# First loads cut and split over two queues, the last gate moved, normed operands and squares moved to VectorE, and a transpose split in a decoder trunk

## The chip, the core and the metric

The kernel runs on one core of a Trainium2 chip. A core has five engines that work side by side and meet at semaphores: TensorE (PE, matmuls and transposes), VectorE (DVE), ScalarE (ACT), GpSimd (POOL) and SyncE (SP, which here only issues DMAs). Data lies in SBUF, matmuls write to PSUM. Each engine runs its own instructions in the order in which they were put in its queue. The metric is the device time of one execution in microseconds.

## What is computed

A two-layer decoder trunk over 256 tokens of width 1024, all in float32: a Mamba-2 layer, a gated FFN with a short causal convolution, dilated attention with a shared K/V, a second such FFN, and a final RMS norm.

```python
x = x + _mamba2_mixer(_rms_norm(x, a_norm[i]), ssm_w_in[i], ...)   # z, x, B, C, dt; conv; SSD; gate; group norm; w_out
x = x + _conv_ffn(_rms_norm(x, ffn_norm[layer]), ffn_w_up[layer], ffn_conv_w[layer], ffn_w_down[layer])
k_sh, v_sh = _shared_kv(x, kv_norm, w_kv, positions)
x = x + _dilated_mixer(_rms_norm(x, b_norm[j]), k_sh, v_sh, att_w_q[j], att_w_o[j], positions)
x = x + _conv_ffn(...)
return _rms_norm(x, final_norm)
```

## The kernel before

The stream X is held transposed, as 8 tiles of 128 channels by 256 tokens. Every float32 matmul is made of three matmuls on rounded parts: an operand is split in a high part (`xh`, `wh`, rounded by a cast) and a low part (`xl`, `wl`, the rest by a subtraction), and the products high-high, low-high and high-low are summed in PSUM (L270 to L272, L290 to L292, L660 to L668). ScalarE makes the casts (L96) and VectorE the subtractions (L98), 1024 columns at a time.

The weights come through the class `Weights`: a fixed sequence of units of 1 MB, three raw buffers, six pairs of `wh` and `wl`, each unit fetched one unit ahead of its use. `begin` (L144) loads the first two units in five pieces (512, 512, 1024, 1024, 1024 columns), with pieces of x between them, all issued by SP. The order on TensorE is written out by hand; on the other engines a scheduler puts the instructions in order ahead of time, by their place in the program and by when it thinks that they are ready, and that order is then fixed.

The stages around the change:

- The start: five pieces of weights and x, `hi_lo` (L184) on each tile of x times the norm's weight, the first matmuls of `z_pair`, then the norm's statistics and dt. `chunk_sums` (L447, tile `pac`) needs a chain of small VectorE operations on dt.
- The Mamba layer: a loop over 8 groups g. In it `conv_mm` for xs and for B and C, and the SSD of earlier groups, each cut in parts: `ssd_b` (transposes `px`), `ssd_a` (`pg`, then `gs` by ScalarE), `ssd_m` (GpSimd multiplies `dec` by `gs`, L531), `ssd_c` (`yo`, `py`, then a chain through VectorE, GpSimd and ScalarE that ends in `y` at L580), and `ssd_d` (transposes of `y` into `pt`, L588, then `hi_lo` into `yy`). The gates of groups 4 to 7 (`z_mm`, L387, in two halves of 24 matmuls, and `z_post`) stand in groups 1, 3, 5 and 7. In group 7 `ssd_d(5)` and `ssd_c(6)` stand between the halves (L630 to L636).
- `res_proj` (L641): w_out, w_down of the first FFN, and w_o. For the first tiles of outputs the last rows of k are put last (`late`), and `hooks` put other work after a given count of steps; a step is three matmuls, for one output tile and one k. When an output tile is done VectorE adds it to X (L680), and `Stream.add` makes the next stage's operands (L187) and adds its square to a sum (`add_sq`, L224).
- The FFNs (`ffn`, L708): 22 tiles of two halves. The first five tiles use operands without the norm's row factor, and the factor is put in afterwards (`u`, L724). From the sixth (j = 5) on, the operands are `normed` (L319, tiles `xnh` and `xnl`). After each tile come the conv steps (L314), the gate (L729) and the split of the result (L734).
- Attention: for each head h three `q_tile`s (24 matmuls each), `p_transpose(h - 2)` between the first and the second, then `values` for a pair of heads, then `scores(h - 1)`. `p_transpose` turns the probabilities in two blocks (c = 0: `p`, two transposes, copied by ScalarE; c = 1: `pm`, three, copied by VectorE).

Of the kernel before, what the change touches and what calls it, by code (L numbers as in the profile page):

```python
# [53 lines left out]
def trunk(ctx, tc, a, out):  # L54
# [17 lines left out]
    def load_x(i):  # L72
        SP.dma_start(out=X[:, 2 * i:2 * i + 2, :], in_=a["x"][:, 2 * i:2 * i + 2, :])
# [27 lines left out]
    class Weights:  # L101
# [42 lines left out]
        def begin(self, load, operand):  # L144

            raw = [wp.tile([128, 2048], F32, tag="raw", bufs=RB, name="raw") for _ in range(2)]
            whl = [[wp.tile([128, 1024], F32R, tag=t, bufs=WB, name=t) for t in ("wh", "wl")]
                   for _ in range(4)]
            cols = [slice(0, 512), slice(512, 1024), slice(1024, 2048), slice(2048, 3072),
                    slice(3072, 4096)]  # L150

            def part(t, c):
                return t[c.start // 2048][:, c.start % 2048:c.start % 2048 + c.stop - c.start]

            for i, c in enumerate(cols):
                if i != 1:
                    load(max(i - 1, 0))
                SP.dma_start(out=part(raw, c), in_=part([q[1] for q in self.seq], c))
            SP.dma_start(out=wdt.rearrange("p k h -> p (k h)"), in_=a["w_dt"])
            for i, c in enumerate(cols):  # L160
                wh, wl = (t[:, c.start % 1024:c.start % 1024 + c.stop - c.start]
                          for t in whl[c.start // 1024])
                if i == 0:
                    operand(0)
                elif i > 1:
                    operand(2 * i - 2)
                ACT.copy(out=wh, in_=part(raw, c))
                DVE.tensor_tensor(out=wl, in0=part(raw, c), in1=wh.bitcast(F32), op=ALU.subtract)
                if i == 0:
                    operand(1)  # L170
                elif i > 1:
                    operand(2 * i - 1)
            self.got += [whl[:2], whl[2:]]
# [10 lines left out]
    def hi_lo(xh, xl, x, w):  # L184

        ACT.activation(out=xh, in_=x, func=AF.Copy, scale=w)
        DVE.scalar_tensor_tensor(out=xl, in0=x, scalar=w, in1=xh.bitcast(F32),  # L187
                                 op0=ALU.mult, op1=ALU.subtract)
# [35 lines left out]
    def add_sq(acc, k):  # L224
        if k == 0:
            ACT.activation(out=acc, in_=X[:, 0, :], func=AF.Square)
        else:
            sq = wk.tile([128, T], F32, tag="sq", name="sq")
            ACT.activation(out=sq, in_=X[:, k, :], func=AF.Square)  # L229
            POOL.tensor_tensor(out=acc, in0=acc, in1=sq, op=ALU.add)  # L230
# [88 lines left out]
    def normed(w, rb):  # L319
# [3 lines left out]
        for k in range(KT):  # L323
            t = wk.tile([128, T], F32, tag="sq", name="xnt")
            ACT.activation(out=t, in_=X[:, k, :], func=AF.Copy, scale=P(w)[:, k:k + 1])
            POOL.tensor_tensor(out=t, in0=t, in1=rb, op=ALU.mult)
            ACT.copy(out=h[:, k, :], in_=t)
            POOL.tensor_tensor(out=l[:, k, :], in0=t, in1=h[:, k, :].bitcast(F32), op=ALU.subtract)
# [21 lines left out]
    W.begin(load_x, lambda k: hi_lo(xh[:, k, :], xl[:, k, :], X[:, k, :], P("a_norm")[:, k:k + 1]))  # L350
# [247 lines left out]
    for g in range(NG):  # L598
# [31 lines left out]
        if g in ZAT:  # L630
            z_mm(ZAT[g], 0)
            if g == NG - 1:
                ssd_d(g - 2)
                ssd_c(g - 1)
            z_mm(ZAT[g], 1)
            z_post(ZAT[g])  # L636
    ssd_b(NG - 1)
# [3 lines left out]
    def res_proj(w, nk, operand, late, S, first=2, hooks={}):  # L641
# [42 lines left out]
        while n0 < KT:  # L684
# [12 lines left out]
            for k in last:  # L697
# [6 lines left out]
    res_proj("w_out", 16, lambda k: yy[k // 2][:, k % 2 * 2:k % 2 * 2 + 2, :], [14, 15], S,  # L704
             first=4, hooks={20: lambda: ssd_d(NG - 2), 24: lambda: ssd_c(NG - 1), 52: lambda: ssd_d(NG - 1)})
# [164 lines left out]
    def q_tile(h, st, g):  # L870
# [3 lines left out]
        tile_a(po[:, g % 2, :], st["us"][g], xh, xl)  # L874
        if g:
# [39 lines left out]
    def p_transpose(h, st):  # L915


        if h % 2 == 0:
            pair[h // 2] = act.tile([128, 2, 640], F32, tag="xh0", name="pts")
        pts = pair[h // 2]  # L920
        for c in range(2):
# [26 lines left out]
    for h in range(AH):  # L948
        q_start(h, hs[h])
        q_tile(h, hs[h], 0)  # L950
        if h > 1:
            p_transpose(h - 2, hs[h - 2])
        q_tile(h, hs[h], 1)
# [216 lines left out]
```

## Time and profile before

| what | value |
|---|---|
| time, median of 3 runs | 779.81 us (777.24 to 781.5) |
| the profiled execution | 777.25 us |
| its span, first to last instruction | 775.5 us |
| TensorE busy | 761.5 us, 98% |
| VectorE busy | 604.4 us, 78% |
| ScalarE busy | 470.1 us, 61% |
| GpSimd busy | 146.2 us, 19% |
| read from HBM | 133.17 MB, 174 GB/s over the span |

A matmul row's duration is longer than the distance to the next matmul, since matmuls are pipelined; so starts are to be compared, not durations. A number in square brackets at the end of a timeline row is the time that the engine stood idle before it, with what ended that time.

### The profile page before, as it was taken

The numbers are of one execution on the slowest core, as the hardware profiler recorded it, in microseconds if no ns is written. First come the engines' busy times: TensorE is split into PE (matmuls) and PEld (weight loads), VectorE is DVE, ScalarE is ACT, GpSimd is POOL, SyncE is SP. The second block draws the span as 40 slices with busy tenths as digits, with TensorE's granted clock in tenths as the row PEclk, the third lists the DMA queues.
The fourth block names the chain that finished last, engine by engine and source line by source line (L and its number), as shares of the span: only waits on it lengthen the run. The fifth ranks groups of instructions, "written<-read, shape, count | busy, mean of one in ns | idle before, by whom it ended". The sixth has DMA issues, their size and how long they took to land.

```text
span 775.5 us, 14630 instructions
## 1 busy us (share of the span) xinstructions
PE 761.5 (98%) x5832; PEld 721.9 (93%) x5832; DVE 604.4 (78%) x1008; ACT 470.1 (61%) x793; POOL 146.2 (19%) x142
## 2 busy tenths in 40 slices
PE   8999999989999999999999999999999999999996
PEld 7899999989989999999888998989999999999885
DVE  5989988887496999887677598777587999888452
ACT  6757777775566676565556446556376767655331
POOL 0003626354216100000111132111125200000000
PEclk9999999999999999999999999999999999999998
DMA  8584753434173565545556554253234565554621
GB/s 308 212 300 170 283 174 110 164 109 158 61 272 110 173 233 202 207 151 173 184 200 236 194 189 147 101 187 118 105 115 158 191 224 212 184 197 141 220 75 54
DMA packets 22772, 135.72 MB, mean 175 GB/s; under 512 B 2544, under 2 KB 3600, under 8 KB 8624
## 3 DMA queue, kind: packets, MB, share of 16 engines
q1 hardware_dynamic: 21216, 130.03, 48.2%
q10 hardware_dynamic: 1488, 4.75, 1.8%
q8 instruction: 46, 0.75, 0.4%
q14 instruction: 22, 0.18, 0.1%
HBM read 133.17 MB, written 1.61 MB: 174 GB/s over the span
## 4 chain that ended last, share of the span: by engine, by line
PE 89%; DVE 4%; issue 2%; ACT 2%; DMA 1%; POOL 1%; SPq 0%; POOLq 0%; DVEq 0%
PE po L270 18%; PE po L271 17%; PE po L272 17%; PE po L660 7%; PE po L668 4%; PE po L662 4%; PE fo L1030 2%; PE fo L1028 2%; PE fo L1029 2%; PE py L565 2%; DVE wl L98 2%; PE po L290 1%; PE po L291 1%; PE po L292 1%; DMA raw<-w_z 1%
## 5 line engine op out<-in xcount | busy, mean ns | idle before, releaser
L98 DVE TENSOR_TENSOR wl<-raw,wh 128x1024 fp32r<-128x1024 f32 (+1 forms) x238 | 296.2, 1250 | 77.9 <-ACT wh L96 73.8
L96 ACT CAST wh<-raw 128x1024 fp32r<-128x1024 f32 (+1 forms) x238 | 245.0, 1040 | 184.3 <-PE po L271 99.1
L270 PE MATMUL po<-xnh,wh 128*128 128x256 f32 x800 | 226.6, 283 | 0.0
L272 PE MATMUL po<-xnh,wl 128*128 128x256 f32 x800 | 226.1, 283 | 0.0
L271 PE MATMUL po<-xnl,wh 128*128 128x256 f32 x800 | 225.3, 282 | 0.0
L270 PEld LDWEIGHTS po<-xnh,wh 128*128 128x128 f32 x800 | 150.9, 189 | 0.4 <-issue 0.2
L271 PEld LDWEIGHTS po<-xnl,wh 128*128 128x128 f32 x800 | 151.0, 189 | 0.0
L272 PEld LDWEIGHTS po<-xnh,wl 128*128 128x128 f32 x800 | 150.1, 188 | 0.1
L270 PE MATMUL po<-xh,wh 128*128 128x256 f32 x400 | 114.7, 287 | 0.0
L271 PE MATMUL po<-xl,wh 128*128 128x256 f32 x400 | 113.0, 282 | 0.5 <-DVE xl L187 0.5
L272 PE MATMUL po<-xh,wl 128*128 128x256 f32 x400 | 113.1, 283 | 0.0
L314 DVE SCALAR_TENSOR_TENSOR cv<-po,prm,cv 128x255 f32<-128x255 f32 (+2 forms) x232 | 106.2, 477 | 5.4 <-ACT cv L310 2.8
L270 PEld LDWEIGHTS po<-xh,wh 128*128 128x128 f32 x400 | 76.1, 190 | 1.6 <-issue 1.5
L271 PEld LDWEIGHTS po<-xl,wh 128*128 128x128 f32 x400 | 76.1, 190 | 0.7 <-DVE xl L187 0.7
L272 PEld LDWEIGHTS po<-xh,wl 128*128 128x128 f32 x400 | 75.8, 190 | 0.0
L660 PE MATMUL po<-gp,wh 128*128 128x512 f32 x176 | 61.4, 392 | 0.0
L230 POOL TENSOR_TENSOR sqacc<-sqacc,sq 128x256 f32<-128x256 f32 x21 | 21.4, 1019 | 211.5 <-ACT sq L229 211.2
L662 PE MATMUL po<-gp,wl 128*128 128x256 f32 x176 | 49.3, 280 | 0.0
L660 PEld LDWEIGHTS po<-gp,wh 128*128 128x128 f32 x176 | 33.0, 187 | 7.5
L1028 PE MATMUL fo<-wh,gp 128*128 128x512 f32 x88 | 34.5, 392 | 0.0
L1030 PE MATMUL fo<-wl,gp 128*128 128x512 f32 x88 | 34.5, 392 | 0.0
L1029 PE MATMUL fo<-wh,gp 128*128 128x512 f32 x88 | 34.5, 392 | 0.0
(226 smaller groups left out, 1283.0 us busy)
## 6 DMA issues: line engine op xcount, KB each, us to landing
raw<-w_up SPq DMA_DIRECT2D x44, 1024.0 KB, 4.8
raw<-w_down SPq DMA_DIRECT2D x18, 1024.0 KB, 4.8
raw<-w_xs SPq DMA_DIRECT2D x8, 1024.0 KB, 6.2
raw<-w_bc SPq DMA_DIRECT2D x8, 1024.0 KB, 5.5
raw<-w_out SPq DMA_DIRECT2D x8, 1024.0 KB, 4.9
raw<-w_q SPq DMA_DIRECT2D x8, 1024.0 KB, 5.1
raw<-w_z SPq DMA_DIRECT2D x6, 1024.0 KB, 6.0
dec<-rows ACTq DMA_DIRECT2D x8, 512.0 KB, 5.3
```

What stands on the lines that cost most here:

```text
L96: ACT.copy(out=wh[:, :n], in_=raw)
L98: DVE.tensor_tensor(out=wl[:, :n], in0=raw, in1=wh[:, :n].bitcast(F32), op=ALU.subtract)
L270: PE.matmul(po, lhsT=wh, rhs=xh, start=start, stop=False, **kw)
L271: PE.matmul(po, lhsT=wh, rhs=xl, start=False, stop=False, **kw)
L272: PE.matmul(po, lhsT=wl, rhs=xh, start=False, stop=stop, **kw)
L314: r = DVE.scalar_tensor_tensor(out=dst[:, i, s:], in0=u[:, i, :T - s], scalar=w[i][:, taps - 1 - s:taps - s], in1=dst[:, i, s:], op0=ALU.m ...
L660: PE.matmul(p.rearrange("p c t -> p (c t)"), lhsT=wh[:, c], rhs=y.rearrange("p c t -> p (c t)"), start=st, stop=False, skip_group_check=True)
L662: PE.matmul(p[:, 1, :], lhsT=wl[:, c], rhs=y[:, 0, :], start=False, stop=sp, skip_group_check=True)
L668: PE.matmul(p[:, o, :], lhsT=l[:, c], rhs=y[:, x, :], start=st and q == 0 and not o, stop=sp and q == 2, skip_group_check=True)
L1028: PE.matmul(po[c], lhsT=x[:, 0, t], rhs=wh[:, o], start=k == 0, stop=False)
L1029: PE.matmul(po[c], lhsT=x[:, 1, t], rhs=wh[:, o], start=False, stop=False)
L1030: PE.matmul(po[c], lhsT=x[:, 0, t], rhs=wl[:, o], start=False, stop=k == FT - 1)
```

## The change

It has four parts. First, x is loaded in pieces of 1, 1, 2, 2, 2 tiles instead of 2, 2, 2, 2, each ahead of its piece of weights, and the first two pieces of weights are issued by ScalarE's queue. The first tile's high part is made by VectorE. Second, both halves of the last gate and its `z_post` stand ahead of `ssd_d(5)` and `ssd_c(6)`, and in w_out four instead of two rows of k are put last, with the hooks of `ssd_c(7)`, `ssd_d(6)` and `ssd_d(7)` moved. Third, `normed` makes its product by one VectorE operation instead of ScalarE's and GpSimd's two, and its low part by VectorE; `add_sq` adds on VectorE. Fourth, `p_transpose` turns its second block after four of the eight k of the second `q_tile`.

```diff
     def load_x(i):
-        SP.dma_start(out=X[:, 2 * i:2 * i + 2, :], in_=a["x"][:, 2 * i:2 * i + 2, :])
+        k = slice(i, i + 1) if i < 2 else slice(2 * i - 2, 2 * i)
+        SP.dma_start(out=X[:, k, :], in_=a["x"][:, k, :])
...
             for i, c in enumerate(cols):
-                if i != 1:
-                    load(max(i - 1, 0))
-                SP.dma_start(out=part(raw, c), in_=part([q[1] for q in self.seq], c))
+                load(i)
+                (SP if i > 1 else ACT).dma_start(out=part(raw, c), in_=part(src, c))
...
-                if i == 0:
-                    operand(0)
-                elif i > 1:
+                if i < 2:
+                    operand(i)
+                else:
                     operand(2 * i - 2)
                 ACT.copy(out=wh, in_=part(raw, c))
                 DVE.tensor_tensor(out=wl, in0=part(raw, c), in1=wh.bitcast(F32), op=ALU.subtract)
-                if i == 0:
-                    operand(1)
-                elif i > 1:
+                if i > 1:
                     operand(2 * i - 1)
...
-    def hi_lo(xh, xl, x, w):
-        ACT.activation(out=xh, in_=x, func=AF.Copy, scale=w)
+    def hi_lo(xh, xl, x, w, dve=False):
+        if dve:
+            DVE.tensor_scalar(out=xh, in0=x, scalar1=w, scalar2=None, op0=ALU.mult)
+        else:
+            ACT.activation(out=xh, in_=x, func=AF.Copy, scale=w)
...
             ACT.activation(out=sq, in_=X[:, k, :], func=AF.Square)
-            POOL.tensor_tensor(out=acc, in0=acc, in1=sq, op=ALU.add)
+            DVE.tensor_tensor(out=acc, in0=acc, in1=sq, op=ALU.add)
...
             t = wk.tile([128, T], F32, tag="sq", name="xnt")
-            ACT.activation(out=t, in_=X[:, k, :], func=AF.Copy, scale=P(w)[:, k:k + 1])
-            POOL.tensor_tensor(out=t, in0=t, in1=rb, op=ALU.mult)
+            DVE.scalar_tensor_tensor(out=t, in0=X[:, k, :], scalar=P(w)[:, k:k + 1], in1=rb,
+                                     op0=ALU.mult, op1=ALU.mult)
             ACT.copy(out=h[:, k, :], in_=t)
-            POOL.tensor_tensor(out=l[:, k, :], in0=t, in1=h[:, k, :].bitcast(F32), op=ALU.subtract)
+            DVE.tensor_tensor(out=l[:, k, :], in0=t, in1=h[:, k, :].bitcast(F32), op=ALU.subtract)
...
-        if g in ZAT:
+        if g in ZAT and g < NG - 1:
             z_mm(ZAT[g], 0)
-            if g == NG - 1:
-                ssd_d(g - 2)
-                ssd_c(g - 1)
             z_mm(ZAT[g], 1)
             z_post(ZAT[g])
+    z_mm(7, 0)
+    z_mm(7, 1)
+    z_post(7)
+    ssd_d(NG - 3)
+    ssd_c(NG - 2)
     ssd_b(NG - 1)
     ssd_a(NG - 1)
     ssd_m(NG - 1)
...
-    res_proj("w_out", 16, lambda k: yy[k // 2][:, k % 2 * 2:k % 2 * 2 + 2, :], [14, 15], S,
-             first=4, hooks={20: lambda: ssd_d(NG - 2), 24: lambda: ssd_c(NG - 1), 52: lambda: ssd_d(NG - 1)})
+    res_proj("w_out", 16, lambda k: yy[k // 2][:, k % 2 * 2:k % 2 * 2 + 2, :], [12, 13, 14, 15], S,
+             first=4, hooks={24: lambda: (ssd_c(NG - 1),), 30: lambda: (ssd_d(NG - 2),), "k12": lambda: (ssd_d(NG - 1),)})
...
         q_tile(h, hs[h], 0)
         if h > 1:
-            p_transpose(h - 2, hs[h - 2])
-        q_tile(h, hs[h], 1)
+            p_transpose(h - 2, hs[h - 2], (0,))
+        q_tile(h, hs[h], 1, range(4))
+        if h > 1:
+            p_transpose(h - 2, hs[h - 2], (1,))
+        q_tile(h, hs[h], 1, range(4, KT))
```

## Rows read from the trace of the kernel before

**Rows 1.** The page, part 4: the chain that ended last, by engine.

```profile
PE 89%; DVE 4%; issue 2%; ACT 2%; DMA 1%; POOL 1%; SPq 0%; POOLq 0%; DVEq 0%
```

**Rows 2.** Waits of PE: who waited for whom: us in total, times, longest.

```profile
PE ptr L924 <- DVE pm L910: 1.4, 4, 0.4
...
PE pac L451 <- DVE smalls L441: 0.6, 1, 0.6
PE po L271 <- DVE xl L187: 0.5, 1, 0.5
```

**Rows 3.** Timeline of 0 to 17 us: start, us, engine, line, op, tiles, [idle before].

```profile
0.73 1.28 ACT L423 ACT_TABLE_LOAD   x1 [0.73 <-PEq L1162]
...
1.63 0.91 SPq L158 DMA_DIRECT2D raw<-w_z  x2
...
12.43 1.05 ACT L167 CAST wh<-raw 128x1024 fp32r<-128x1024 f32 x1 [0.39 <-DMA raw<-w_z]
...
14.79 0.19 PEld L292 LDWEIGHTS poz<-wl,xh 128*128 128x128 f32 x1 [0.56 <-DVE wl L168]
```

**Rows 4.** Busy time by stretch: PE, PEld, DVE, ACT, POOL; clock; DMA share, GB/s.

```profile
1.00:4.00 3.00, 2.95 (x14) 2.95 (x15) 0.19 (x2) 1.24 (x2) 0.00 (x0) 1.00 0.49 155
4.00:14.40 10.40, 9.29 (x32) 6.96 (x31) 6.19 (x10) 8.32 (x16) 1.29 (x1) 1.00 0.99 338
...
566.00:584.00 18.00, 17.54 (x147) 17.33 (x146) 18.00 (x24) 14.42 (x27) 6.34 (x7) 1.00 0.51 172
588.00:609.00 21.00, 21.00 (x175) 20.91 (x174) 16.43 (x26) 15.89 (x33) 13.39 (x16) 1.00 0.33 114
```

**Rows 5.** Timeline of PE, 168.9 to 181.4 us.

```profile
171.70 0.28 PE L292 MATMUL po<-wl,xnh 128*128 128x256 f32 x1
174.07 0.95 PE L588 MATMUL pt<-cst,y 128*128 128x128 f32 x4 [2.09 <-ACT y L580]
...
176.00 1.55 PE L565 MATMUL py<-xdt,dec 128*128 128x64 f32 x12 [0.16 <-POOL dec L531]
177.36 0.36 PE L290 MATMUL po<-wh,xnh 128*128 128x256 f32 x1
...
180.29 0.60 PE L542 MATMUL px<-cst,cv 128*128 128x128 f32 x4
...
181.30 0.37 PE L668 MATMUL po<-yy,wh 128*128 128x256 f32 x1
```

**Rows 6.** Timelines of ACT and of POOL, 145 to 210 us.

```profile
173.51 0.91 ACT L580 ACTIVATE y<-y,rs 128x256 f32<-128x256 f32 x2 [0.26 <-POOL rs L578]
...
185.40 3.53 POOL L531 TENSOR_TENSOR dec<-dec,gs 128x512 f32<-128x512 f32 x2 [0.98 <-ACT gs L524]
```

**Rows 7.** Timelines of PE (487.5 to 492.5) and of DVE (464 to 496).

```profile
488.01 0.38 PE L924 MATMUL ptr<-cst,p 128*128 128x128 f32 x2
488.80 0.52 PE L924 MATMUL ptr<-cst,pm 128*128 128x128 f32 x3 [0.40 <-DVE pm L910]
...
489.62 0.54 DVE L926 COPY pts<-ptr 128x384 f32<-128x384 f32 x1
```

**Rows 8.** Groups of DVE by form, 236 to 262: busy us, mean ns.

```profile
L314 DVE SCALAR_TENSOR_TENSOR cv<-u,prm,cv 128x254 f32<-128x254 f32 x6 | 5.1, 877 | 0.0
```

**Rows 9.** Timeline of DVE, 18 to 48 us.

```profile
30.40 0.48 DVE L343 SCALAR_TENSOR_TENSOR xnt<-X,prm,rbc 128x256 f32<-128x256 f32 x1
```

**Rows 10.** Groups of DVE by form, 566 to 584.

```profile
L187 DVE SCALAR_TENSOR_TENSOR xl<-X,prm,xh 128x256 fp32r<-128x256 f32 x8 | 6.6, 833 | 0.0
L680 DVE TENSOR_TENSOR X<-po,X 128x256 f32<-128x256 f32 x8 | 3.1, 415 | 2.4 <-PE po L668 2.4
```

**Rows 11.** Timelines of ACT (239 to 262), DVE (605 to 610), PE (607.9 to 608.9).

```profile
256.56 0.41 ACT L327 CAST xnh<-xnt 128x256 fp32r<-128x256 f32 x1 [1.32 <-POOL xnt L326]
...
607.33 1.22 DVE L98 TENSOR_TENSOR wl<-raw,wh 128x1024 fp32r<-128x1024 f32 x1
...
608.60 0.39 PE L272 MATMUL po<-xnh,wl 128*128 128x256 f32 x1
```

More of the change, by code (lines that the diff above doesn't have):

```diff
@@ L153, in part @@
                 return t[c.start // 2048][:, c.start % 2048:c.start % 2048 + c.stop - c.start]
+            src = [q[1] for q in self.seq]
             for i, c in enumerate(cols):
-                if i != 1:
-                    load(max(i - 1, 0))
-                SP.dma_start(out=part(raw, c), in_=part([q[1] for q in self.seq], c))
+                load(i)
+                (SP if i > 1 else ACT).dma_start(out=part(raw, c), in_=part(src, c))
             SP.dma_start(out=wdt.rearrange("p k h -> p (k h)"), in_=a["w_dt"])
@@ L348, in operands @@
         return h, l
-    W.begin(load_x, lambda k: hi_lo(xh[:, k, :], xl[:, k, :], X[:, k, :], P("a_norm")[:, k:k + 1]))
+    W.begin(load_x, lambda k: hi_lo(xh[:, k, :], xl[:, k, :], X[:, k, :], P("a_norm")[:, k:k + 1], k == 0))
     W.fetch(3)
@@ L868, in q_start, with q_tile @@
         st["us"] = W.get("w_q", h, 0) + W.get("w_q", h, 1)
-    def q_tile(h, st, g):
+    def q_tile(h, st, g, ks=range(KT)):
         if g != 1:
@@ L873, in q_tile @@
         po = st["po"]
-        tile_a(po[:, g % 2, :], st["us"][g], xh, xl)
-        if g:
+        tile_a(po[:, g % 2, :], st["us"][g], xh, xl, ks=ks)
+        if g and ks[-1] == KT - 1:
             gs = slice(0, 2) if g == 1 else slice(2, 3)
@@ L913, in trunk, with p_transpose @@
     pair = {}
-    def p_transpose(h, st):
-        if h % 2 == 0:
+    def p_transpose(h, st, cs=(0, 1)):
+        if h % 2 == 0 and cs[0] == 0:
             pair[h // 2] = act.tile([128, 2, 640], F32, tag="xh0", name="pts")
         pts = pair[h // 2]
-        for c in range(2):
+        for c in cs:
             pt = ps.tile([128, 512], F32, tag=f"t{3 + c}", name="ptr")
```

## The prediction, made before the change was run

> **What bounds the kernel now.** I read the chain of work that ended last first: 89% of it is TensorE and 4% VectorE, so time can only come out of places where TensorE stands still [rows 1]. The second view is therefore the list of what TensorE waited for. It is short: beside the long stall at the last gate (below) it has four waits of the probabilities' transposes (`ptr`) for `pm`, one of `pac` at 44 us and one of a matmul on `xl` of 0.5 us [rows 2]. That list counts a gap from the modelled end of a matmul, so I take the price of a stall from starts in the timeline instead. The changed parts sit on these stalls and on the start; no edit removes a matmul. One level step is useful: half a gate (24 matmuls) runs from 177.36 to 180.29, 2.93 us, so one 256-column matmul takes 0.122 us [rows 5].
>
> **First loads.** At 14.79 TensorE waits for the `wl` of the fourth piece of weights, whose cast starts at 12.43 when its DMA lands [rows 3]. So the fourth piece's landing sets the end of this stage, and not the first matmul. The DMA engines are 0.49 busy from 1 to 4 us and 0.99 busy after [rows 4]: first the single issuing queue limits, then the transfers do. The change moves two weight issues to ScalarE's queue and adds one x load, so on SP the fourth piece moves up by one issue, 0.91 / 2 = 0.46 us [rows 3]. That is also the value I take, 0.5. Filling the 3 us from 0.49 to 0.99 would be 1.5 us, the far end. The other end is a loss: ScalarE begins at 0.73 with a table load of 1.28 us [rows 3], and if its two issues stand behind it the first piece comes about half a microsecond later than now. The first normed operand goes to VectorE; this moves the first matmul only, which isn't the limit, and costs nothing. What is late next is `pac`, which already waits 0.6 us for VectorE [rows 2]; VectorE's chain there starts from TensorE's own results, so I let the gain pass.
>
> The row says 0.99 busy after 4 us. The Trainium skill (DMA: Bandwidth & Descriptors, Issuing engines are not separate DMA queues) speaks against a larger gain: queues of different engines run on the same 16 DMA engines, and a second one saves issue time only. By that rule the far end of 1.5 falls away and the half microsecond stays; the trace agrees as far as it goes.
>
> **The last gate whole ahead of group 5's turning.** Now the second half of gate 7 stands behind `ssd_d(5)` and `ssd_c(6)`. TensorE's last matmul of the first half starts at 171.70, the transposes of `ssd_d(5)` at 174.07; less 0.12 that is 2.25 us of stall for `y` of group 5, which ScalarE ends at 173.51 + 0.91 = 174.42 [rows 5, 6]. The four transposes behind the stall take 0.95 us where the four of `px` take 0.60: 0.35 more [rows 5]. With the second half put first, TensorE is busy until 171.82 + 2.93 = 174.75, when `y` is there: both go. The third loss is `py`, whose fifth matmul starts at 176.00 when `dec` is there [rows 5]. It could have started four transposes, two `yo` and four `py` after 174.07 + 0.35, at 174.42 + 0.44 + 0.43 + 0.45 = 175.74: 0.26 lost. After the change the same count from 174.75 gives 176.07, so `dec` is there and this goes too. The sum is 2.25 + 0.35 + 0.26, say 2.8 us. `z_post` only moves up and hides beside matmuls.
>
> `w_out` then starts at 178.5 instead of 181.30. Its first three units are split ahead of that; group 6 is now wanted after 48 steps instead of 37, which covers the later `ssd_d(6)`. What is late next is `ssd_c(7)`: 24 steps of 3 matmuls, 8.8 us, put it at 187.3. Its `dec` came from GpSimd at 185.40 + 3.53 = 188.93 [rows 6]. That multiply waits for `gs`, which comes from `ssd_a(7)`, now 2.8 us earlier, so it should move along. If it doesn't, 1.6 us are given back. I take none; bounds 1.2 to 2.9 us gained.
>
> **Probabilities turned in two places.** In head 3 the first block's transposes start at 488.01, the second block's at 488.80; two transposes take 0.22, so 0.57 us are lost for `pm`, of which the list shows 0.40 [rows 7]. The list has four such waits with 1.4 us [rows 2]: three like this one and one with 0.2. With the 0.17 that the list leaves out of each, it is 3 x 0.57 + 0.37 = 2.1 us. After the change 12 matmuls, 1.46 us, stand between the two blocks, more than twice the wait. The other side of the cover: VectorE's copy of the second block (489.62 for 0.54 [rows 7]) is needed by `values`, now 24 matmuls behind it, from then on 12. From the end of the turned block, 488.23 + 1.46 + 0.33 = 490.0, to `values` at 491.5 there are 1.5 us for 0.54. If VectorE takes a split first, 1.2 us by [rows 11], 0.3 is lost, in three heads 0.9. I take 2.1 and keep 1.2 as the low end. A further switch between kinds of matmul is added per head; at 180.29 transposes follow a gate's matmuls with no gap [rows 5], so I price it at nothing.
>
> **Normed operands and squares on VectorE.** In each FFN GpSimd loses eight multiplies and eight subtractions and ScalarE eight scalings. VectorE gains 8 x (0.48 + 0.42) = 7.2 us: the multiply is the row of L343, the subtraction the mean of L680, both 128x256 [rows 9, 10]. It also gets something back. While GpSimd works, VectorE's operations are longer: six conv steps of 128x254 average 0.877 us between 236 and 262, where one of the same kind and size takes 0.48; that is 2.4 us from this group alone [rows 8, 9]. So the load grows by at most 4.8 us, and VectorE has 21.00 - 16.43 = 4.6 us idle in the like stretch of the second FFN [rows 4]. It just fits, with a thin cover: the `wl` of tile 5 ends at 607.33 + 1.22 = 608.55, and the matmul that reads it starts at 608.60 [rows 11]. For the change speaks that ScalarE stood 1.32 us at 256.56 for GpSimd's multiply with weight casts queued behind [rows 11]; that wait goes. Against it: the subtraction on VectorE now waits for ScalarE's cast, splits and conv steps are queued behind it on VectorE, and TensorE waits for the splits. I take 0.25 us lost in each FFN; bounds 0.1 gained and 3 lost.
>
> The squares: in the last projection VectorE is busy 18.00 of 18 us, and TensorE loses 0.5 us for the last `xl` [rows 2, 4]. Eight `xl` take 0.833 each instead of 0.48, so 2.8 us come back [rows 9, 10]; of seven additions of 0.42 six stand ahead of the last `xl`, 2.5. The difference is 0.3; I take 0.4 gained, since a stretched split comes back too. Bounds 0.6 either way. In the other two projections TensorE never waited, and matmuls hide the additions; uncovered they are 2.9 us each.
>
> The rows show VectorE's operations up to twice as long beside GpSimd's. The Trainium skill (SBUF — State Buffer, Who interferes with whom) says that a VectorE instruction with two SBUF inputs and a GpSimd instruction that reads SBUF exclude each other for the whole instruction. By that rule GpSimd's own time comes back to VectorE and its load would not grow; that belongs to the third rival. The trace bears out the lengthening, not the full amount.
>
> **The sum.** 0.5 + 2.8 + 2.1 + 0.4 - 0.5 = 5.3 us. The profiled execution took 777.25 us (span 775.5 and 1.75 around it), which would become 772.0. The median of the three runs is 2.56 above the profiled one; the three spread over 4.3 us, and nothing in the profile prefers an end, so I take the gain off the median: 779.8 - 5.3 = 774.5.
>
> **Rivals.** First, half is given back: `ssd_c(7)` waits 1.6 for `dec`, the start gains nothing (0.5), `values` waits 0.9. The gain is 2.3, the time 777.5. For it: each new cover is 1 to 1.5 us thick. Against it: GpSimd's multiply follows `ssd_a`, which moves too.
>
> Second, VectorE becomes the bound in the FFNs; this is the slow side. The subtractions wait for ScalarE and tile 5's split comes late. TensorE feels it as soon as VectorE is 0.05 us later at 608.5 than now. The other edits gain 5.8, so it decides from 2.9 us in each FFN, and beyond the measurable from 4.9. At 3 in each the time is 780.0; with no relief and no idle time used, 7.2 each, it is 779.8 + 14.4 - 5.8 = 788.4.
>
> Third, the loads gain the full 1.5 and the FFNs 0.1 each: 7.0, 772.8. It needs full DMA engines from 1 us on.
>
> Last, the start does not do what it says, ScalarE issuing behind its table load: 0.5 lost instead of gained, 775.5, inside the forecast's spread.
>
> **How the numbers follow.** The forecast with its spread (773 to 776.5) gets 0.52, half given back 0.25, VectorE as the bound 0.15, the larger gain 0.08. A measurement of this kernel can tell about 0.5% from no change, 3.9 us: 775.9 and 783.7. Faster: 0.08 and nearly all of 0.52 make 0.58 (some of the spread lies above 775.9). Slower: over half of 0.15, 0.09. The rest, 0.33, is the same. The range reaches from the larger gain on the profiled execution's footing, 770.5, to the mild form of VectorE's bound, 781.
>
> **What would show it.** Right: no wait of `pt` at 172, `w_out` starting about 3 us sooner, no wait of `ptr`, conv steps near 0.48 at the start of both FFNs, no `xl` wait after the last projection. Wrong: TensorE waiting for `wl` or `xnl` near 256 to 262 or 605 to 612, for `dec` near 187, for `pts` ahead of `values`, or `pac` waiting longer by what the start gained.

## The result and the profile after

The changed kernel takes 771.69 us (median of five, 771.42 to 773.9) against 779.81 us; the ratio is 0.9899 with an interval of 0.9877 to 0.992. It is faster, as forecast, and inside the range; the time forecast was 774.5 us, with a spread of 773 to 776.5, and the measured time lies 1.3 us below that spread. By medians the gain is 8.1 us, between the two profiled executions only 5.6 us (777.25 to 771.69). The forecast was 5.3. The distance between 5.6 and 8.1 is the main question of what follows.

The engine shares of the chain of work that ended last, of the kernel after [rows 1]:

```profile
PE 93%; issue 2%; DVE 2%; ACT 1%; DMA 1%; POOL 1%; SPq 0%; POOLq 0%; DVEq 0%
```

The waits of TensorE after [rows 2]: who waited for whom, us in total, times, longest.

```profile
PE warm L90 <- DVE nhalf L269: 1.1, 1, 1.1
PE poz L293 <- ACT wh L169: 0.8, 1, 0.8
PE poz L295 <- DVE wl L170: 0.7, 2, 0.5
PE pac L454 <- DVE smalls L444: 0.7, 1, 0.7
PE poz L293 <- DVE xh L187: 0.4, 1, 0.4
PE pg L522 <- ACT cv L419: 0.3, 1, 0.3
PE po L673 <- DVE OT L950: 0.2, 1, 0.2
```

The waits of `pt`, `ptr`, `xl` and of `py` for `dec` are gone, as forecast; `pac` still waits, and `pg` for `cv` is new. The new wait stands between the transposes `px` and `w_out` in TensorE's timeline (start, us, line, tiles, idle before in brackets) [rows 5]:

```profile
174.34 0.60 PE L591 MATMUL pt<-cst,y 128*128 128x128 f32 x4
...
177.13 0.61 PE L545 MATMUL px<-cst,cv 128*128 128x128 f32 x4
178.06 0.70 PE L522 MATMUL pg<-cv 128*128 128x256 f32 x2 [0.33 <-ACT cv L419]
...
178.74 0.48 PE L673 MATMUL po<-yy,wh 128*128 128x256 f32 x2
```

ScalarE's timeline says why: three weight casts stand in its fixed order ahead of the `cv` that `pg` reads [rows 6].

```profile
174.18 2.94 ACT L98 CAST wh<-raw 128x1024 fp32r<-128x1024 f32 x3
177.02 0.47 ACT L189 ACTIVATE yy<-pt,prm 128x256 fp32r<-128x256 f32 x1
177.39 0.62 ACT L419 ACTIVATE cv<-cv 128x512 f32<-128x512 f32 x1
```

Starts of the same TensorE instruction in the two profiled executions give the gain stage by stage:

| TensorE starts | before | after | gained so far | in this stage |
|---|---|---|---|---|
| `pac` | 44.29 | 43.98 | 0.31 | 0.31 |
| last gate, first matmul | 168.92 | 168.62 | 0.30 | 0 |
| `w_out`, first matmul | 181.30 | 178.74 | 2.56 | 2.26 |
| first matmul behind `vo` and `ss`, after the first FFN | 430.31 | 427.57 | 2.74 | 0.18 |
| w_o, step behind the last `ptr` but one | 551.16 | 546.19 | 4.97 | 2.23 |
| `ss` after w_o | 584.44 | 578.75 | 5.69 | 0.72 |
| `pxt`, the first turning of X for the output, in the second FFN | 619.98 | 614.16 | 5.82 | 0.13 |

So in the profiled executions the start gave 0.3 of a forecast 0.5, the gate 2.3 of 2.8, the turning 2.2 of 2.1, the squares 0.7 of 0.4 and the stages of the two FFNs 0.18 and 0.13 instead of a loss of 0.25 each. That adds up to 5.8, as the spans show (775.5 to 769.6 is 5.9), and not to the 8.1 of the medians.

### The profile page after: what moved, and what is told of

It reads as the page before. It is cut to its first block, busy times and chain, and to the rows that moved or that the text cites. A ratio compares the mean times of both kernels' runs of the same rounds, so it can differ in the third digit from the quotient of the medians.

```text
span 769.6 us, 14590 instructions
## 1 busy us (share of the span) xinstructions
PE 758.8 (99%) x5832; PEld 720.5 (94%) x5832; DVE 605.4 (79%) x1062; ACT 461.3 (60%) x776; POOL 97.7 (13%) x89
## 4 chain that ended last, share of the span: by engine, by line
PE 93%; issue 2%; DVE 2%; ACT 1%; DMA 1%; POOL 1%; SPq 0%; POOLq 0%; DVEq 0%
PE po L273 18%; PE po L275 18%; PE po L274 18%; PE po L665 7%; PE po L673 6%; PE po L667 4%; PE fo L1036 2%; PE fo L1037 2%; PE fo L1038 2%; PE py L568 1%; PE po L293 1%; PE po L294 1%; PE po L295 1%; PE s L903 1%; PE s L896 1%
## 5 line engine op out<-in xcount | busy, mean ns | idle before, releaser
L251 POOL TENSOR_TENSOR rcol<-ms,nhalf 128x2 f32<-128x2 f32 x5 | 6.4, 1282 | 274.5 <-DVE ms L248 274.5
```

## Experiments: each part undone by itself

All four start from the changed kernel, which took 771.69. Its own executions spread from 771.42 to 773.9, and the kernel before took 779.81, 780.48, 780.16 and 780.19 by the medians of the four sets of executions that are compared here. So a difference of half a microsecond between two medians is not shown by the medians alone.

**The first loads undone.** x in four pieces and all first loads from SP again:

```diff
-        k = slice(i, i + 1) if i < 2 else slice(2 * i - 2, 2 * i)
-        SP.dma_start(out=X[:, k, :], in_=a["x"][:, k, :])
+        SP.dma_start(out=X[:, 2 * i:2 * i + 2, :], in_=a["x"][:, 2 * i:2 * i + 2, :])
...
-                (SP if i > 1 else ACT).dma_start(out=part(raw, c), in_=part(src, c))
+                SP.dma_start(out=part(raw, c), in_=part([q[1] for q in self.seq], c))
```

> The changed kernel with the first part undone: x in four pairs, all first loads on SP, the first high part on ScalarE. Theory, from the two profiled executions: every milestone up to the last gate stands only 0.3 us earlier after the change (chunk_sums' first matmul 44.29 to 43.98), so this kernel loses 0.3 us of the changed kernel's 771.7: 772.0, with a spread of its own no larger than the changed kernel's. Rival: the medians differ by 8.1 us but the profiled executions by 5.6, and the kernel before spreads over 4.3 us where the changed one spreads over 2.5. If the missing 2.5 us belong to the start, where the DMA engines are full and landings can differ from run to run, this kernel comes out 2 to 3 us slower than the changed one, 774 to 775, and spreads over about 4 us.

Measured: 772.25 us (772.04 to 773.54), 0.56 more than with the part. In its list of TensorE's waits the casts of the first pieces carry 2.7:

```profile
PE poz L293 <- ACT wh L167: 2.7, 2, 1.4
```

The changed kernel has 0.8 there, but so has the kernel before, whose first loads are the same as here; so this sum differs between executions of the same loads and does not measure the part. The start of `pac` is the better sign: 44.54 instead of 43.98, with the same wait of 0.65 ahead of it. VectorE's chain moves with TensorE, and the gain of the start reaches the end of the program. It is not clear of chance: with the new loads `pac` starts between 43.80 and 44.03 in six of the profiled kernels and at 44.59 in a seventh (the one with the squares alone undone, below), with the old loads at 44.29 and 44.54.

**The last gate undone.** The two halves stand around `ssd_d(5)` and `ssd_c(6)` again, with the old `late` and hooks:

```diff
+        if g in ZAT:
             z_mm(ZAT[g], 0)
+            if g == NG - 1:
+                ssd_d(g - 2)
+                ssd_c(g - 1)
             z_mm(ZAT[g], 1)
...
-    z_mm(7, 0)
-    z_mm(7, 1)
-    z_post(7)
-    ssd_d(NG - 3)
-    ssd_c(NG - 2)
```

> The changed kernel with the second part undone: the last gate's second half behind the turning of group 5, and the old late rows and hooks of w_out. Theory: the part is worth what the traces show between the gate's first matmul and the first of w_out, 12.38 us before and 10.12 after, 2.26 us; this kernel takes 774.0, and its profile shows the wait of the turned block for the normalised output of group 5 near 172 us, 2.1 us, again, and no wait of pg for the activation of group 7. Rival (half given back later): w_out hides part of it anyway, and the loss is under 1.2 us.

Measured: 776.6 us (773.47 to 779.12, ten executions; ratio to before 0.9946, 0.9928 to 0.9963). The part is worth 4.9 us, twice what the stages say. The stall for `y` is back in TensorE's timeline, and two matmuls of the gate's second half behind it start 0.22 apart:

```profile
173.82 0.95 PE L591 MATMUL pt<-cst,y 128*128 128x128 f32 x4 [2.09 <-ACT y L583]
...
178.90 0.41 PE L295 MATMUL po<-wl,xnh 128*128 128x256 f32 x1
179.12 0.41 PE L293 MATMUL po<-wh,xnh 128*128 128x256 f32 x1
```

The stretches around the gate (length, then busy us of PE, PEld, DVE, ACT, POOL, then the granted clock, DMA share, GB/s) show what the forecast had not counted:

```profile
174.00:176.00 2.00, 1.93 (x11) 1.54 (x11) 1.42 (x4) 1.63 (x4) 1.70 (x2) 0.82 0.00 0
176.00:178.00 2.00, 2.00 (x11) 2.00 (x11) 0.61 (x2) 1.02 (x2) 0.00 (x0) 0.50 0.00 0
178.00:180.00 2.00, 2.00 (x11) 2.00 (x11) 0.87 (x3) 0.00 (x0) 0.73 (x1) 0.50 0.00 0
180.00:182.00 2.00, 2.00 (x11) 2.00 (x11) 1.78 (x2) 0.94 (x1) 1.22 (x1) 0.50 0.00 0
182.00:184.00 2.00, 2.00 (x18) 1.95 (x17) 1.86 (x3) 1.15 (x6) 0.92 (x1) 0.97 0.62 102
```

TensorE is fully busy from 176 to 182, yet it does 11 matmuls in 2 us instead of 18: the granted clock is 0.50, the 1.2 GHz level. What stands ahead of it is the stall for `y`. The same stretches of the profiled execution of before, which had the same stall of 2.09 [rows 5]:

```profile
176.00:178.00 2.00, 2.00 (x17) 2.00 (x18) 1.20 (x3) 1.02 (x2) 0.00 (x0) 1.00 0.00 0
178.00:180.00 2.00, 2.00 (x19) 2.00 (x18) 1.54 (x4) 1.05 (x1) 0.97 (x2) 1.00 0.00 0
```

There the clock stayed at 1.00. So the same stall has a fall of the clock behind it in one execution and none in another, and the one execution of before that was profiled is one without the fall.

**Squares and normed operands undone.** Both go back to GpSimd and ScalarE:

```diff
-            DVE.tensor_tensor(out=acc, in0=acc, in1=sq, op=ALU.add)
+            POOL.tensor_tensor(out=acc, in0=acc, in1=sq, op=ALU.add)
...
-            DVE.scalar_tensor_tensor(out=t, in0=X[:, k, :], scalar=P(w)[:, k:k + 1], in1=rb,
-                                     op0=ALU.mult, op1=ALU.mult)
+            ACT.activation(out=t, in_=X[:, k, :], func=AF.Copy, scale=P(w)[:, k:k + 1])
+            POOL.tensor_tensor(out=t, in0=t, in1=rb, op=ALU.mult)
```

and the subtraction likewise.

> The changed kernel with the third part undone: normed operands and squares on GpSimd and ScalarE again. Theory: the two profiled executions put 0.5 us on the last xl after the third projection and some 0.4 us on waits at the first tile with normed operands in the two FFNs; this kernel takes 772.6 and the xl wait near 579 us (0.5) is back. My prediction's side: VectorE pays for the normed operands, 0.25 us in each FFN, so this kernel would lose nothing or gain 0.1: 771.6. Rival: the part also takes away a wait that differs from run to run, and is worth 2 us or more: 773.7.

Measured: 772.25 us (772.14 to 772.55), 0.56 more. The wait after the last projection is back in the list:

```profile
PE po L274 <- DVE xl L190: 0.5, 1, 0.5
```

**The turning undone.** Both blocks of `p_transpose` stand again between the first and the second `q_tile`.

```diff
-            p_transpose(h - 2, hs[h - 2], (0,))
-        q_tile(h, hs[h], 1, range(4))
-        if h > 1:
-            p_transpose(h - 2, hs[h - 2], (1,))
-        q_tile(h, hs[h], 1, range(4, KT))
+            p_transpose(h - 2, hs[h - 2])
+        q_tile(h, hs[h], 1)
```

> The changed kernel with the fourth part undone: both blocks of the probabilities turned between the first and second q tile. Theory: 2.1 to 2.2 us lost, 773.9, with four waits of the transposes for pm in the profile, 1.4 us in the list. Rival: the waits for pm came from VectorE's order in the kernel before and are smaller now that other parts changed; under 1 us lost.

Measured: 773.89 us (773.66 to 775.99), 2.2 more, with the old wait in the list:

```profile
PE ptr L929 <- DVE pm L915: 1.4, 4, 0.4
```

The four differences are 0.56, 4.9, 0.56 and 2.2, together 8.2, where the whole change gave 8.1. The parts add up, though with two of them no larger than the spread of a kernel it is luck that they do so to 0.1. Of the 2.8 that the forecast lacked 2.1 lie in the gate, and most of the rest in the third part, for which 0.1 of loss was forecast.

The traces part the stages more finely than the medians. The time between the same starts on TensorE, us:

| stage | before | changed | loads undone | gate undone | squares and normed undone | turning undone |
|---|---|---|---|---|---|---|
| up to `pac` | 44.29 | 43.98 | 44.54 | 44.03 | 43.92 | 43.82 |
| `pac` to `w_out` | 137.01 | 134.76 | 134.77 | 139.92 | 134.75 | 134.77 |
| `w_out` to behind the first FFN | 249.01 | 248.83 | 248.82 | 248.82 | 248.99 | 248.83 |
| from there to `ss` after w_o | 154.13 | 151.18 | 151.18 | 151.18 | 151.91 | 153.42 |
| `ss` to `pxt` | 35.54 | 35.41 | 35.42 | 35.42 | 35.51 | 35.67 |

Behind `pac` a part that is undone changes its own stage and leaves the others the same to 0.02 us, but for the last row, which moves by up to 0.3 without a cause that shows. So by the traces the gate without a fall of the clock is worth 2.25 (137.01 to 134.76), the gate undone with the fall costs 5.16, the turning is worth 2.24, and the third part 0.73 in the stage of the last projection and 0.16 in the stage of the first FFN.

## Experiments: what the stall at the gate costs

**The stall filled.** To part the stall from the clock, the kernel with the gate undone gets ten matmuls on a tile of ones ahead of `ssd_d(5)`. Their result is used by nothing; they only keep TensorE at work while it would wait for `y` (the trace lists the ten as x20).

```diff
             if g == NG - 1:
+                fill = ps.tile([128, 512], F32, tag="t4", name="fill")
+                for i in range(10):
+                    PE.matmul(fill[:, :128], lhsT=ones, rhs=ones, start=True, stop=True)
                 ssd_d(g - 2)
```

> The kernel without the second part, with ten matmuls of 128x128 on a tile of ones put on TensorE between the first half of the last gate and the turning of group 5; their results are not used. They fill most of the 2.1 us in which TensorE waits there and take nothing away from the wait itself, which ends when the normalised output of group 5 is there. Theory: without the second part most executions took 776.6 and two of ten 773.5 to 773.9, because TensorE, having stood idle 2.1 us, runs at the lower of its two clocks (granted 0.50) from 175.3 to 182.1 us in the profiled execution. With TensorE kept busy the clock stays, and this kernel takes 773.7 to 774.1 in all its executions, granted clock 0.998 or above. Rival: the 2.6 us beyond the wait come from the rest of the part (the late rows and hooks in w_out): then it stays at 776.5 with the same spread.

Measured: 773.73 us (773.45 to 775.03). More work on TensorE, and 2.87 us less than 776.6. In TensorE's timeline the fill covers the wait, and the gate's second half runs at its full pace, 0.12 between starts, where the kernel with the bare stall has 0.21 to 0.22:

```profile
171.47 2.40 PE L638 MATMUL fill<-ones 128*128 128x128 f32 x20
173.72 0.95 PE L591 MATMUL pt<-cst,y 128*128 128x128 f32 x4
...
177.20 0.28 PE L294 MATMUL po<-wh,xnl 128*128 128x256 f32 x1
177.32 0.28 PE L295 MATMUL po<-wl,xnh 128*128 128x256 f32 x1
```

So by the medians the gate's 4.9 us are 2.04 for the stall and what lies around it (773.73 - 771.69) and 2.87 for the clock behind it. The traces part them in one stage: from `pac` to the first matmul of w_out (43.93 to 180.94) the filled kernel takes 137.01 us, exactly what before takes without a fall, against 134.76 with the part and 139.92 with the bare stall and the fall. That is 2.25 for the stall and 2.91 for the clock. The mean granted clock of each execution agrees: of the ten with the gate undone, the two at 0.999 took 773.47 and 773.85, the eight at 0.992 to 0.994 took 776.5 to 779.12. Of 40 executions of before, run beside these kernels, nine had 0.997 to 0.999 and took 776.9 to 777.8, the other 31 had 0.990 to 0.995 and took 778.9 to 783.7. In both kernels the middles of the two groups lie 3.1 us apart. The profiled one, at 777.25, belongs to the nine; the median lies among the 31. No trace of before with the fall exists; that its 31 slower executions have it at the gate is concluded from the same stall, the same distance and the lower clock, and why it comes in one execution and not in the next stays open.

Two of the five executions of the changed kernel took 773.3 and 773.9 at 0.997. What slowed them no trace shows; this stays open. A mean of 0.997 alone shows no fall that costs time: the mean counts the end of the program too, and in the profiled execution of before (0.997) the clock is below 1.00 only behind the last matmul, in the last 5 us.

## Experiments: the small terms

**Squares alone undone**, the normed operands left on VectorE:

```diff
-            DVE.tensor_tensor(out=acc, in0=acc, in1=sq, op=ALU.add)
+            POOL.tensor_tensor(out=acc, in0=acc, in1=sq, op=ALU.add)
```

> The changed kernel with the additions of the squares on GpSimd again; the normed operands stay on VectorE. Theory: the whole third part is worth 0.56 us by the medians, and the profile without it shows 0.5 us for the last xl of the third projection; that wait belongs to the squares. So this kernel loses 0.5 (772.2, xl wait of 0.5 us near 579), and the normed operands alone are worth nothing that can be measured, under 0.2, though VectorE took 8 x 0.9 us of work from GpSimd in each FFN. Rival (my prediction's shares): the squares are worth 0.4 and the normed operands cost 0.5, so with the normed operands alone the kernel would be 0.4 us slower than the changed one and 0.1 us faster than... the changed kernel minus its squares stands at 772.1 either way; the two are told apart against the kernel without the whole part, 772.25: theory 772.2, rival 772.75.

Measured: 772.28 us (771.83 to 773.46). That is 0.59 more, as much as both together (0.56), and the `xl` wait of 0.5 is back. So the squares carry this part and the normed operands give nothing that the medians show. The difference is no larger than the spread of either kernel; the trace is the firmer sign. From behind the first FFN to `ss` after w_o this kernel takes 151.91 us, as with both undone, against 151.18 with them: 0.73 for the squares. The stage of the first FFN takes 248.83, as in the changed kernel, where the kernel with both undone takes 248.99: 0.16 gained by the normed operands.

**One queue.** The pieces of x as in the change, but all loads issued by SP:

```diff
-                (SP if i > 1 else ACT).dma_start(out=part(raw, c), in_=part(src, c))
+                SP.dma_start(out=part(raw, c), in_=part(src, c))
```

> The changed kernel with all first loads issued by SP again, x still in five pieces. My prediction's step: the queue is what limits before 4 us, and SP's slots decide when the fourth piece lands; then this kernel, with two more issues ahead of that piece on SP, gives back the 0.5 us, 772.2, and its fourth piece lands 0.5 to 0.9 us later than 10.98. Rival: in the changed kernel SP issued the fourth piece at 4.49, later than before (4.01), and yet it landed earlier (10.98 against 12.41), so issue slots don't decide; then this kernel takes 771.7 as the changed one, and the landing differs by less than 0.3.

Measured: 772.66 us (772.32 to 773.37), 1.0 more than with two queues and 0.4 more than with the whole part undone; in the profiled executions `pac` starts at 45.41, against 43.98 and 44.54. Neither expectation held: SP issues the fourth piece at the same time as in the changed kernel (4.48 and 4.49), and it lands 1.6 us later, at 12.6 instead of 11.0. So it is not that piece's own slot that decides. What differs ahead of it is that the first piece of weights goes out at 1.64 instead of 0.74 and the third at 3.53 instead of 2.59. Stretches of 4 to 9 us of the kernel with one queue, then of the changed kernel (last two columns DMA share and GB/s) show the DMA engines partly idle with one queue:

```profile
4.00:9.00 5.00, 3.67 (x15) 2.10 (x14) 2.43 (x6) 2.17 (x4) 0.00 (x0) 1.00 0.71 243
```

```profile
4.00:9.00 5.00, 4.38 (x18) 3.24 (x17) 3.40 (x8) 2.78 (x6) 0.00 (x0) 1.00 0.98 351
```

**Two waits attacked at once.** What the changed kernel still waits for, `pac` (0.7) and `pg` (0.3), was to be covered: `chunk_sums` with its two decay loads behind the second half of B and C in group 0, and `ssd_a(7)` with `ssd_m(7)` behind two steps of `w_out`.

```diff
         conv_mm(g, "bc", 0)
-        if g == 0:
-            chunk_sums()
-            decay_load(0)
-            decay_load(1)
...
         conv_mm(g, "bc", 1)
+        if g == 0:
+            chunk_sums()
+            decay_load(0)
+            decay_load(1)
...
-    ssd_a(NG - 1)
-    ssd_m(NG - 1)
...
-             first=4, hooks={24: lambda: (ssd_c(NG - 1),),
+             first=4, hooks={2: lambda: (ssd_a(NG - 1), ssd_m(NG - 1)), 24: lambda: (ssd_c(NG - 1),),
```

> The changed kernel with two of the waits that are left moved: chunk_sums stands behind the second half of B and C of group 0 instead of the first, so that the 0.8 us at 44 us which TensorE waits for VectorE's small operations are covered by 24 matmuls; and ssd_a(7) with ssd_m(7) stands behind two steps of w_out, so that the 0.6 us at 178 us for group 7's activation are covered. Theory: both covers hold and nothing behind is late, since the decays are needed two groups later and GpSimd's multiply for group 7 had 3 us to spare: 771.7 - 1.4 = 770.3. Rival: VectorE's chain there, which ends the first wait, is late for the next thing as well (the decay rows go out to memory and come back), and the time stays at 771.2 or above.

Measured: 773.9 us (772.77 to 775.92, nine executions), slower than the changed kernel. Both waits are gone, and the list has a new one at the top. Behind it the granted clock is 0.56 and 0.59 in the stretches of 110 to 112 and 112 to 114 us:

```profile
PE po L273 <- DVE cv L317: 1.9, 1, 1.9
```

**Each move alone.** First `ssd_a(7)` and `ssd_m(7)` only, then `chunk_sums` only.

> The changed kernel, with ssd_a(7) and ssd_m(7) put behind the first two steps of w_out; nothing else is moved. Six matmuls then stand ahead of pg, 0.7 us, and the wait of pg for cv was 0.3 in the list and 0.5 to 0.6 by starts. Theory (the wait of pg is a plain term of TensorE's chain): the wait goes, 771.7 - 0.5 = 771.2 us, no fall of the granted clock, no wait of po L273 for cv near 107 us. Rival (the new wait of the kernel with both moves came from this move, through the fixed order of the other engines): over 773 us, with a wait of one of the next operands for VectorE or ScalarE near 108 or 177 us.

Measured: 771.28 us (770.95 to 771.67, six executions; ratio to before 0.9891, 0.9874 to 0.9908). `pg` starts with no idle time ahead of it:

```profile
178.10 0.60 PE L522 MATMUL pg<-cv 128*128 128x256 f32 x2
```

This is the best kernel here, by 0.4 us in the median and 0.8 in the span (768.8 to 769.6, of which 0.18 lies ahead of `pac`); the intervals of the two ratios overlap.

> The changed kernel, with chunk_sums and its two decay loads put behind the second half of B and C of group 0; nothing else is moved. Theory (this move it was that put the conv step of 128x253 behind two splits on VectorE): pac waits no more, 0.7 us, but po waits for cv near 107 us for about 1.9, and the granted clock falls behind it in most executions: 773.0 to 775. Rival (the two moves only did it together): the wait near 107 us is gone too and the time is 771.7 - 0.7 = 771.0 us.

Measured: 774.41 us (772.85 to 775.18). The loss is this move's. VectorE's timeline shows the `cv` that TensorE waits for behind two splits, stretched to 1.48 and 1.92:

```profile
104.97 1.48 DVE L100 TENSOR_TENSOR wl<-raw,wh 128x1024 fp32r<-128x1024 f32 x1
...
106.76 1.92 DVE L100 TENSOR_TENSOR wl<-raw,wh 128x1024 fp32r<-128x1024 f32 x1
108.60 0.47 DVE L317 SCALAR_TENSOR_TENSOR cv<-po,prm,cv 128x253 f32<-128x253 f32 x1
```

TensorE's timeline and the stretches behind it show the second stall of about 2 us, at another place of the kernel, and the clock behind it again:

```profile
109.22 0.36 PE L273 MATMUL po<-xnh,wh 128*128 128x256 f32 x1 [2.04 <-DVE cv L317]
```

```profile
108.00:110.00 2.00, 0.78 (x5) 0.81 (x6) 2.00 (x3) 0.17 (x1) 0.00 (x0) 0.90 0.87 360
110.00:112.00 2.00, 2.00 (x11) 2.00 (x10) 1.29 (x2) 2.00 (x4) 0.00 (x0) 0.50 0.81 209
112.00:114.00 2.00, 2.00 (x15) 2.00 (x15) 1.27 (x2) 2.00 (x4) 0.00 (x0) 0.74 0.95 377
```

Worked out: 2.04 of stall, less the 0.65 that `pac` waited, plus 15 matmuls from 109.65 to 112.86 at 0.21 instead of 0.12 (1.4), gives 2.8. In the trace the transposes behind this place start 2.98 later than in the changed kernel (113.65 and 110.67). The whole profiled execution is 3.4 longer (773.0 to 769.6); 0.5 of that is lost in the second FFN, between `ss` and `pxt`. The medians differ by 2.7.

## Why the prediction was right, and where it was wrong

**The last gate** was the right mechanism and the term of the sum that was mis-sized: 2.8 forecast, 4.9 measured by the undone part. The step that failed is the price of the stall as its length plus two small losses. Its length is in the trace; what TensorE's clock does behind it is not in the one execution that was read, and is, by their mean clocks, in most others. Without the fall the part gave 2.25, less than the 2.8, since `pg` now starts 0.5 late for `cv`, a wait that the forecast had not looked for: it followed `dec`, not ScalarE's queue of casts.

**The base.** The forecast said that nothing in the profile prefers the profiled execution or the median, and took the gain off the median. What gave it 774.5 was 779.8 - 5.3, a median that contains the fall of the clock less a gain that does not. The same sum on the profiled execution gave 772.0, and that was 0.3 off. The 2.56 between the two was itself the missing term; the clock fall measured as 2.87. That 772.0 came so near is in part luck: the gate's 0.5 too much stands against some 1 us too little for the third part. The measured time also lies below the forecast's own spread and nearest to the rival of a larger gain, which had a chance of 0.08; it is in the range because the range was drawn down to that rival on the profiled execution's footing (777.25 - 7.0 is 770.25, where the prediction writes 770.5).

**The first loads**: 0.5 forecast, 0.56 measured in the medians and 0.31 to 0.56 in the traces, by a way that was wrong, so that the size is luck. The list of waits in before also had these two, which the prediction passed over when it named the fourth piece as what ends the stage:

```profile
PE poz L290 <- ACT wh L167: 0.8, 1, 0.8
PE poz L292 <- DVE wl L168: 0.3, 1, 0.3
```

They belong to the first and the third piece. By starts the wait for the fourth, at 14.79, cost only 0.30 (14.79 - 14.26, less the step of 0.23), so 0.5 could not come from it alone. And in the kernel with the loads undone, which loads as before does, the chain that ended last runs through a piece of x, landing at 7.87, and not through the fourth piece of weights: which piece ends the stage differs between two executions. The forecast also had the fourth piece land earlier because SP issues it one slot sooner. In the trace of after SP issues it later than in before and its cast still starts earlier, 11.35 against 12.43 [rows 3]. First the issue in before, then the rows of after:

```profile
4.01 0.45 SPq L158 DMA_DIRECT2D raw<-w_z  x1
```

```profile
4.49 0.33 SPq L160 DMA_DIRECT2D raw<-w_z  x1
...
9.07 1.04 ACT L169 CAST wh<-raw 128x1024 fp32r<-128x1024 f32 x1 [0.96 <-DMA raw<-w_z]
...
11.35 1.04 ACT L169 CAST wh<-raw 128x1024 fp32r<-128x1024 f32 x1
```

What now sets the end of the stage is the third piece, for which ScalarE stands idle for 0.96; the landing of the fourth makes nobody wait. From 4 to 14.4 us the DMA engines are 1.00 busy and move 377 GB/s, where they moved 338 at 0.99 [rows 4]:

```profile
4.00:14.40 10.40, 8.46 (x33) 6.00 (x33) 7.39 (x14) 8.11 (x15) 0.61 (x1) 1.00 1.00 377
```

So a share near 1 did not mean that nothing more could be moved. The Trainium skill (DMA: Bandwidth & Descriptors, Issuing engines are not separate DMA queues) allows a second queue the issue time only. The kernel with one queue agrees: with the smaller pieces the single queue left the engines 0.71 busy from 4 to 9 us, where before, with one queue and larger pieces, had 1.00. The higher rate at a full share does not need the second queue: from 9 to 14.4 us the kernel with one queue moves 403 GB/s at a share of 1.03 and the changed kernel 401 at 1.01, where the two with the old loads move 350 and 351 at 0.98. Whether the sizes of the pieces make it, or which transfers fall into that stretch, no run parts.

**The turning**: 2.1 forecast, 2.2 measured. Starts from the timeline, and not the 1.4 of the list, were the right price.

**Normed operands and squares**: 0.1 of loss forecast, 0.56 of gain measured in the medians and 0.9 in the spans (770.5 to 769.6). The step that failed is the FFNs' loss of 0.25 each: the first FFN's stage gained 0.16, the second's lost nothing, and the squares gave 0.73 for a forecast 0.4. The loss was to come from VectorE's load growing by up to 4.8 us in each. At the start of the two FFNs VectorE is indeed busier, 24.83 us from 233.5 to 259.5 against 22.33 from 236 to 262 in before, and 20.56 from 582 to 603 against 16.43 from 588 to 609, but it also gets more operations done there (53 against 32, 46 against 26), and TensorE never waited for it. What came back is in the operations: the conv steps of the first FFN [rows 8] and the last `xl` [rows 10] fell to the 0.48 that one of the kind takes [rows 9]. Groups of VectorE by form, 233.5 to 259.5, then 563 to 579, after:

```profile
L317 DVE SCALAR_TENSOR_TENSOR cv<-u,prm,cv 128x254 f32<-128x254 f32 x8 | 3.7, 478 | 0.0
L328 DVE SCALAR_TENSOR_TENSOR xnt<-X,prm,rbc 128x256 f32<-128x256 f32 x8 | 3.6, 478 | 0.0
...
L331 DVE TENSOR_TENSOR xnl<-xnt,xnh 128x256 fp32r<-128x256 f32 x8 | 3.2, 419 | 0.0
```

```profile
L190 DVE SCALAR_TENSOR_TENSOR xl<-X,prm,xh 128x256 fp32r<-128x256 f32 x8 | 3.7, 477 | 0.0
L233 DVE TENSOR_TENSOR sqacc<-sqacc,sq 128x256 f32<-128x256 f32 x7 | 2.9, 417 | 0.0
```

Over the whole program it is plainer. The busy times of the kernel with this part undone, of the one with the squares alone undone, then of the changed kernel:

```profile
PE 758.8 (98%) x5832; PEld 720.2 (93%) x5832; DVE 604.5 (78%) x1009; ACT 469.0 (61%) x792; POOL 145.6 (19%) x142
```

```profile
PE 758.9 (98%) x5832; PEld 720.4 (93%) x5832; DVE 606.6 (79%) x1041; ACT 462.1 (60%) x776; POOL 119.1 (15%) x110
```

```profile
PE 758.8 (99%) x5832; PEld 720.5 (94%) x5832; DVE 605.4 (79%) x1062; ACT 461.3 (60%) x776; POOL 97.7 (13%) x89
```

VectorE does 53 operations more, 16 x 0.478 + 16 x 0.419 + 21 x 0.417 = 23.1 us by the rows above, and is busy 0.9 us longer: the normed operands make it 2.1 longer, over both FFNs together, and the squares 1.2 shorter. The other 22 came back from its own operations, while GpSimd was relieved of 48 us. The Trainium skill (SBUF — State Buffer, Who interferes with whom) has a VectorE instruction with two SBUF inputs and a GpSimd instruction that reads SBUF exclude each other. The forecast had drawn from it that the load would not grow, and had kept that out of the sum because one group showed less; over the whole program the runs side with the page to within 0.9 us.

**The rivals.** Half given back: `dec` for `ssd_c(7)` ended at 183.9 instead of 188.93 [rows 6], as its multiply followed `ssd_a`, and neither `dec` nor `pts` appears in the list. VectorE as the bound: no `xnl` in the list, and `wl` only at the start of the program. The larger gain came near in time (772.8), about right on the FFNs and wrong on the loads, which gave 0.56 and not 1.5; the clock, which made up the difference, is in no rival. The start behind the table load: ScalarE's first issues start at 0.74 and the table load follows at 1.66.

## What to carry to other kernels

Price a stall of TensorE by its length and by the pace of the matmuls behind it, and compare the mean granted clock of the profiled execution with that of the other executions first: where they differ by more than the end of the program can make, the trace may lack a term that the median has. When work moves between VectorE and GpSimd, count the stretched operations that shrink again, over the whole program. A move that covers a small wait on TensorE can reorder another engine's fixed queue and open a larger wait elsewhere, so try such moves one at a time.

## What the runs showed of the hardware

After an idle time of 2.04 to 2.09 us of TensorE, which was busy before it, the granted clock was 0.50 for some microseconds of full work: in the kernel with the gate undone 11 matmuls in each 2 us from 176 to 182, in the one with `chunk_sums` moved 11 from 110 to 112. With both waits attacked the idle time was 1.86, and the clock fell too. The profiled execution of before had the same idle time and kept 1.00, so whether the clock falls differs between executions of one kernel. The price of a fall, 2.87 us in the medians and 2.91 in the traces of the stage, was larger than that of the idle time ahead of it. With ten useless matmuls in that time the profiled execution shows no fall, and five of six executions took 773.45 to 773.85; the sixth, 775.03 at 0.996, has no trace.
